# Attention masks of a decoder trunk: added by VectorE in place in PSUM instead of by matmuls with an identity

## Chip, cores and metric

The kernel runs on one core of a Trainium2 chip. The metric is the time of one execution on the device in microseconds (us), lower is better. Engines are named as the profile names them: PE is TensorE (PEld its weight loads), DVE is VectorE, ACT is ScalarE, POOL is GpSimd, SP is SyncE, which issues the DMAs.

## What is computed

A decoder trunk of four layers on 256 tokens of width 1024, in float32. Each layer has a token mixer and a SwiGLU feed-forward, both between RMS norms with a residual. The mixers are differential attention (layers 0 and 3), stick-breaking attention (layer 1) and sliding-window attention with sinks (layer 2). Cut to what matters here, the masks:

```
# layers 0 and 3: two softmaxes per head, causal
sc = einsum('bqhcd,bkhcd->bhcqk', qb, k) * scale
p = softmax(where(kpos <= qpos, sc, -inf), axis=-1)
wts = p[:, :, 0] - lam * p[:, :, 1]

# layer 1: stick-breaking, strictly causal
z = einsum('bqhd,bkhd->bhqk', qb, k) * scale
log_1m_beta = where(kpos < qpos, log_sigmoid(-z), 0.0)
suffix = cumsum(log_1m_beta, reverse=True) - log_1m_beta
a = where(kpos < qpos, exp(log_sigmoid(z) + suffix), 0.0)

# layer 2: a window of 128 keys, with a sink per head in the denominator
sc = where(in the window and in the sequence, sc, -inf)
m = maximum(max(sc), sink);  p = exp(sc - m)
probs = p / (sum(p) + exp(sink - m))
```

## The kernel before

**Streams.** The 256 tokens are two streams of 128 rows, `s` = 0 and 1, each a Python generator that goes through all layers (`stream`). Stream 1 attends to its own block of keys and to that of stream 0 (`nk = s + 1` blocks); stream 0 to its own alone.

**Weights.** Weights come from HBM in units of 128x1024 f32 (`load_dma`, tile `stage`). `split` makes two tiles of each: `hi` by ScalarE (rounded to f32r) and `lo` = stage - hi by VectorE. Projections multiply `hi` and `lo` by the split activations in three products (`project`, `rows_product`). Both streams use the same unit from a ring of 11; stream 0 may be at most 8 units ahead (`LAG`), and the splits are emitted 3 units ahead of use (`AHEAD`).

**The order of the work.** `Emitter` is a planner that writes the program in one order. It keeps a clock `em.t` that only matmuls and transposes advance (`mm`, `transpose`). A generator can yield `("d", ns)`: what follows is emitted only when that much TensorE work has been emitted, so the result of another engine is there by then. It can yield `("e", key)` to wait for an event and `("w",)` for a weight unit. Attention work is spawned as tasks (`turned`, `scores`, `values`, in layer 2 `keys` and `heads`) between the projections. From the first layer of stream 1 on, instructions are no longer kept in program order (`act.on = dve.on = pool.on = pe.on = False`), so each engine's final order may differ from the emitted one.

**A score step.** A step covers four score matrices, two `p` by two `j`, from queries and keys of 64 rows each. `score_banks` takes two PSUM banks of the stream (`tag="acc"`, two buffers), one for each `j`. `score_products` multiplies queries and keys for two `p`, all key blocks and both `j` (f32, 64 rows, 128 columns each) into them, then adds the mask. In PSUM, `start=True` on a bank's first matmul clears it, later ones add. The mask is 0 or -1e30 in bf16 (`masks`: causal, strict, before), and one bf16 matmul per bank and masked block with the identity `identb` adds it for both `p` at once. Layers 0, 1 and 3 mask only a stream's own block, layer 2 masks the other one too (`before`).

**After the scores.** In layers 0 and 3 VectorE takes the negated maximum (`nm`), ScalarE the exponentials with their sums (`e`, four instructions), VectorE combines the two softmaxes (`w`), TensorE transposes them (`tw`), ScalarE copies (`wT`), TensorE multiplies by the values (`pv`). In layer 1 ScalarE reads the scores directly with two sigmoids (`f`, `b`), VectorE scans and multiplies (`s`, `b`), TensorE transposes (`ta`). Layer 2 is like layer 0 with one softmax and a sink (`nm`, `es`, `e`, `l`, `tpr`, `pT`). The line that matters in all of them is the delay between a step and its transposes, 3500 ns in layers 0, 1 and 3, 6000 ns in layer 2.

Of the kernel before, what the change touches and what calls it, by code (L numbers as in the profile page):

```python
# [9 lines left out]
F32 = mybir.dt.float32  # L10
F32R = mybir.dt.float32r
BF16 = mybir.dt.bfloat16
I32 = mybir.dt.int32
AF = mybir.ActivationFunctionType
ALU = mybir.AluOpType
# [3 lines left out]
P = 128  # L19
# [138 lines left out]
def trunk_kernel(ctx, tc, x, positions, norm_gains, a_w_in, a_w_out, a_lambda, a_subln, b_w_in, b_w_out,  # L158
                 c_w_in, c_w_out, c_sinks, w_gate, w_up, w_down, out, depth=DEPTH):
    nc = tc.nc  # L160
    cst = ctx.enter_context(tc.tile_pool(name="cst", bufs=1))
# [6 lines left out]
    def bank(tag, s, shape, name):  # L168
        return ps.tile(shape, F32, tag=f"{tag}{s}", name=name, bufs=BANKS[tag])
# [16 lines left out]
    act, dve, pool, pe = (Start(e) for e in (nc.scalar, nc.vector, nc.gpsimd, nc.tensor))  # L186
# [106 lines left out]
    pool.memset(mhalf, -0.5)  # L293
    ident = cst.tile([P, P], F32, name="ident")
    make_identity(nc, ident)
    identb = cst.tile([P, P], BF16, name="identb")
    pool.tensor_copy(identb, ident)

    masks = {n: cst.tile([P, P], BF16, name=f"mask_{n}") for n in ("causal", "strict", "before")}
    for n, op, sign in (("causal", ALU.is_ge, 1), ("strict", ALU.is_gt, 1), ("before", ALU.is_gt, -1)):  # L300
# [72 lines left out]
    def mm(o, a, b, start, stop, f32=False):  # L373
        pe.matmul(o, a, b, start=start, stop=stop)
        n = 1
        for d in o.shape[1:]:
            n *= d
        em.t += n * COLUMN_NS * (4 if f32 else 1)
# [6 lines left out]
    def transpose(o, i):  # L385
        pe.transpose(o, i, ident)
        em.t += P * COLUMN_NS * 4
# [157 lines left out]
    def score_banks(s, n, name):  # L545
        return [bank("acc", s, [P, 2, n], f"sc_{name}{j}") for j in range(2)]

    def score_products(s, sc, q, k, mask):

        for p in range(2):  # L550
            for kb in range(s + 1):
                for j in range(2):
                    hs = slice(64 * j, 64 * j + 64)
                    mm(sc[j][:, p, kb * P:(kb + 1) * P], q(p)[hs], k(p, kb)[hs], p == 0 and kb == 0, False, True)
        for j in range(2):
            kbs = [kb for kb in range(s + 1) if mask(kb) is not None]
            for kb in kbs:
                mm(sc[j][:, :, kb * P:(kb + 1) * P], identb, mask(kb).unsqueeze(1).to_broadcast([P, 2, P]), False, kb == kbs[-1])

    def two_groups(s, name):  # L560
        return [[wk.tile([P, 4, P], F32R, tag=f"o{p}{s}", name=f"o{p}_{name}{g}") for p in "hl"] for g in range(2)]
# [11 lines left out]
    def layer_a(s, i, xn):  # L573
        inst = i // 3
        name = f"a{i}{s}"
# [18 lines left out]
        def scores(g):  # L594
            yield ("e", (name, "q", g))
            if s:
                yield ("e", (f"a{i}0", "k", g))
            yield ("d", 700)
            wT[g] = wk.tile([P, 4, nk, P], F32, tag=f"wT{s}", name=f"wT_{name}{g}", bufs=1)
            l = st[g] = sm.tile([P, 2, 4], F32, tag=f"l{s}", name=f"l_{name}{g}", bufs=2)  # L600
            el = st[g, "el"] = sm.tile([P, 4], F32, tag=f"el{s}", name=f"el_{name}{g}", bufs=2)
            ws = {}
            for step in range(3):
                if step < 2:
                    h0 = 2 * step
                    hs = slice(h0, h0 + 2)
                    sc = score_banks(s, nk * P, f"{name}{g}{h0}")
                    score_products(s, sc, lambda p: qT[g][:, h0 + p, :], lambda p, kb: kT[g, kb][:, h0 + p, :],
                                   lambda kb: masks["causal"] if kb == s else None)
                    nm = sm.tile([P, 2, 2], F32, tag=f"nm{s}", name=f"nm_{name}{g}{h0}")  # L610
                    e = [wk.tile([P, 2, nk * P], F32, tag="t2k", name=f"e{c}_{name}{g}{h0}", bufs=TMP) for c in range(2)]
                    if step:
                        em.set((name, "s", g))
                    for c in range(2):
                        dve.tensor_reduce(nm[:, c, :], sc[c], AX.X, ALU.max, negate=True)
                    for c in range(2):
                        for h in range(2):
                            act.activation(e[c][:, h, :], sc[c][:, h, :], AF.Exp, bias=nm[:, c, h:h + 1],
                                                 accum_out=l[:, c, h0 + h:h0 + h + 1])
                    r = sm.tile([P, 2], F32, tag=f"rl{s}", name=f"rl_{name}{g}{h0}")  # L620
                    dve.reciprocal(r, l[:, 1, hs])
                    dve.scalar_tensor_tensor(r, r, nlam[:, inst:inst + 1], l[:, 0, hs], ALU.mult, ALU.mult)
                    w = ws[step] = wk.tile([P, 2, nk * P], F32, tag=f"as{s}", name=f"w_{name}{g}{h0}", bufs=STEPS)
                    for h in range(2):
                        dve.scalar_tensor_tensor(w[:, h, :], e[1][:, h, :], r[:, h:h + 1], e[0][:, h, :], ALU.mult, ALU.add)
                    yield ("d", 3500)
                if step > 0:
                    if step == 2:
                        yield ("d", 1500)
                    tp = bank("tp", s, [P, 2, nk, P], f"tw_{name}{g}{step}")  # L630
                    for h in range(2):
                        for kb in range(nk):
                            transpose(tp[:, h, kb, :], ws[step - 1][:, h, kb * P:(kb + 1) * P])
                    act.activation(wT[g][:, 2 * step - 2:2 * step], tp, AF.Copy)
                    yield ("d", 300)
            lv = l[:, 0, :]
            dve.scalar_tensor_tensor(el, lv, EPS, lv, ALU.mult, ALU.mult)
            em.set((name, "w", g))
# [41 lines left out]
    def layer_b(s, i, xn):  # L680
        name = f"b{i}{s}"
# [19 lines left out]
        def scores(g):  # L701
            yield ("e", (name, "q", g))
            if s:
                yield ("e", (f"b{i}0", "k", g))
            yield ("d", 700)
            aT[g] = wk.tile([P, 4, 2, nk, P], F32, tag=f"wT{s}", name=f"aT_{name}{g}", bufs=1)
            as_ = {}
            for step in range(3):
                if step < 2:
                    p0 = 2 * step  # L710
                    sc = score_banks(s, n, f"{name}{g}{p0}")
                    score_products(s, sc, lambda p: qT[g][:, p0 + p, :], lambda p, kb: kT[g, kb][:, p0 + p, :],
                                   lambda kb: masks["strict"] if kb == s else None)
                    b, f, sm = [], [], []
                    for j in range(2):
                        f.append(wk.tile([P, 2, n], F32, tag="t2k", name=f"f{j}_{name}{g}{p0}", bufs=TMP))
                        sm.append(wk.tile([P, 2, n], F32, tag="t2k", name=f"s{j}_{name}{g}{p0}", bufs=TMP))
                        b.append(wk.tile([P, 2, n], F32, tag=f"as{s}", name=f"b{j}_{name}{g}{p0}", bufs=STEPS))
                        pool.memset(f[j][:, :, n - 1:n], 0.0)
                    for j in range(2):  # L720
                        act.activation(f[j][:, :, 0:n - 1], sc[j][:, :, 1:n], AF.Sigmoid, scale=-SCALE)
                        act.activation(b[j], sc[j], AF.Sigmoid, scale=SCALE)
                    for j in range(2):
                        for p in (1, 0):
                            dve.tensor_tensor_scan(sm[j][:, p, ::-1], f[j][:, p, ::-1],
                                                         reset[:, 256 - n:256][:, ::-1], 0.0, ALU.mult, ALU.max)
                        dve.tensor_tensor(b[j], b[j], sm[j], ALU.mult)
                    as_[step] = b
                    if step:
                        em.set((name, "s", g))  # L730
                    yield ("d", 3500)
                if step > 0:
                    if step == 2:
                        yield ("d", 1500)
                    for p in range(2):
                        tp = bank("tp", s, [P, 2, nk, P], f"ta_{name}{g}{2 * step - 2 + p}")
                        for j in range(2):
                            for kb in range(nk):
                                transpose(tp[:, j, kb, :], as_[step - 1][j][:, p, kb * P:(kb + 1) * P])
                        act.activation(aT[g][:, 2 * step - 2 + p], tp, AF.Copy)  # L740
                        yield ("d", 300)
            em.set((name, "w", g))
# [31 lines left out]
    def layer_c(s, i, xn):  # L774
        name = f"c{i}{s}"
# [18 lines left out]
        def heads(chunk, g):  # L794
# [13 lines left out]
            sc = score_banks(s, n, f"{name}{g}")  # L808
# [18 lines left out]
            dve.reciprocal(l, l)  # L827
            for j in range(2):
                dve.tensor_tensor(e[j], e[j], l[:, j, :].unsqueeze(2).to_broadcast([P, 2, n]), ALU.mult)
            yield ("d", 6000)  # L830
            for p in range(2):
                tp = bank("tp", s, [P, 2, nk, P], f"tpr_{name}{g}{p}")
                for j in range(2):
# [119 lines left out]
```

## Time and profile before

| | |
|---|---|
| time, median of 3 runs | 1204.88 us (1204.61 to 1205.26) |
| profiled execution, time | 1205.73 us |
| profiled execution, span | 1203.9 us |
| instructions | 16738 |
| granted TensorE clock | 0.998 of full speed |
| PE busy | 1185.8 us |
| DVE busy | 779.2 us |
| ACT busy | 656.9 us |
| POOL busy | 48.1 us |
| HBM read | 203.76 MB |

The span runs from the first to the last instruction of the program; the execution's own time is 1.83 us longer. Busy times are sums over the whole span. Matmuls are pipelined, and their ends in the profile are modelled, so a matmul's cost is better read from the distance between starts than from its own length. The helper that issues the instructions has one line (L181), so instructions are told apart by the tiles that they write and read: `sc_a<-mask_causal,identb` is a mask matmul in layers 0 and 3, where the letter after the underscore is the kind of layer.

### The profile page before, as it was taken

What the parts mean: (1) busy time and instruction counts of PE and PEld (TensorE: products, weight loads), DVE (VectorE), ACT (ScalarE), POOL (GpSimd) and SP (SyncE); (2) the same over time, 40 slices, a digit from 0 to 9 for tenths busy, and PEclk for the clock granted to TensorE, in tenths of its full rate; (3) what the DMA queues carried; (4) which work ended last, traced back from release to release, by engine and by line L of the source; (5) the groups of instructions that cost most, each with busy time, mean ns of one, the idle gap of its engine ahead of it and who ended that gap; (6) DMA issues with size and microseconds to landing.
All of it is one profiled execution on the core that took longest, in us unless ns stands there. A gap on an engine that the chain in (4) does not pass through costs nothing.

```text
span 1203.9 us, 16738 instructions
## 1 busy us (share of the span) xinstructions
PE 1185.8 (98%) x6028; PEld 971.6 (81%) x6028; DVE 779.2 (65%) x1217; ACT 656.9 (55%) x1197; POOL 48.1 (4%) x141
## 2 busy tenths in 40 slices
PE   8999999999999999999999999999999999999997
PEld 7787888888878888888888778888888788888886
DVE  7876765555847666555588666655587776655553
ACT  5665644444756665444476655444475565544442
POOL 2000100000200000000000000000010001000000
PEclk9999999999999999999999999999999999999999
DMA  8635465565644546656664246555565453566550
GB/s 280 206 120 159 151 192 186 189 192 179 225 139 123 176 140 193 191 181 189 192 199 135 88 144 191 191 189 187 185 205 156 129 175 123 179 189 192 180 170 35
DMA packets 140838, 205.90 MB, mean 171 GB/s; under 512 B 9554, under 2 KB 104916, under 8 KB 140756
## 3 DMA queue, kind: packets, MB, share of 16 engines
q1 hardware_dynamic: 140048, 204.51, 54.0%
q8 instruction: 47, 0.77, 0.3%
q10 hardware_dynamic: 708, 0.34, 0.1%
q14 instruction: 35, 0.29, 0.1%
HBM read 203.76 MB, written 1.05 MB: 170 GB/s over the span
## 4 chain that ended last, share of the span: by engine, by line
PE 90%; DVE 3%; ACT 3%; issue 2%; POOL 1%; DMA 1%; ACTq 0%; DVEq 0%; POOLq 0%
PE mm_f L181 39%; PE acc_f L181 18%; PE acc_a L181 3%; PE mm_c L181 2%; PE acc_b L181 2%; PE sc_a L181 2%; PE th_f L181 2%; DVE lo L181 1%; PE acc_c L181 1%; PE sc_b L181 1%; DMA stage<-in_a_w_in_dram 1%; ACT hi L181 1%; PE pv_a L181 1%; PE sc_c L181 1%; PE pv_c L181 1%
## 5 line engine op out<-in xcount | busy, mean ns | idle before, releaser
L181 DVE TENSOR_TENSOR lo<-stage,hi 128x1024 fp32r<-128x1024 f32 x378 | 461.0, 1223 | 285.5 <-ACT hi L181 283.6
L181 ACT ACTIVATE hi<-stage 128x1024 fp32r<-128x1024 f32 x378 | 399.5, 1061 | 324.1 <-PE mm_f L181 154.4
L181 PE MATMUL mm_f<-hi,xh_q 128*128 128x512 f32 x704 | 280.2, 398 | 0.0
L181 PE MATMUL mm_f<-lo,xh_q 128*128 128x512 f32 x704 | 274.5, 390 | 0.0
L181 PE MATMUL mm_f<-hi,xl_q 128*128 128x512 f32 x704 | 217.4, 390 | 1.0 <-DVE xl_q L181 1.0
L181 PEld LDWEIGHTS mm_f<-hi,xl_q 128*128 128x128 f32 x704 | 132.2, 188 | 30.4 <-DVE xl_q L181 1.9
L181 PEld LDWEIGHTS mm_f<-hi,xh_q 128*128 128x128 f32 x704 | 132.2, 188 | 26.1 <-ACT xh_q L181 0.2
L181 PEld LDWEIGHTS mm_f<-lo,xh_q 128*128 128x128 f32 x704 | 132.4, 188 | 25.8
L181 PE MATMUL acc_f<-hi,hTh_f 128*128 128x512 f32 x352 | 113.7, 399 | 0.5 <-ACT hTh_f L181 0.5
L181 PE MATMUL acc_f<-hi,hTl_f 128*128 128x512 f32 x352 | 111.4, 392 | 0.5 <-DVE hTl_f L181 0.4
L181 PE MATMUL acc_f<-lo,hTh_f 128*128 128x512 f32 x352 | 110.7, 390 | 0.0
L181 ACT ACTIVATE t_f<-mm_f,half_f 128x256 f32<-128x256 f32 x88 | 41.7, 474 | 79.7 <-PE mm_f L181 79.7
L181 PEld LDWEIGHTS acc_f<-hi,hTl_f 128*128 128x128 f32 x352 | 65.9, 188 | 14.9 <-DVE hTl_f L181 1.0
L181 PEld LDWEIGHTS acc_f<-lo,hTh_f 128*128 128x128 f32 x352 | 66.1, 188 | 14.0
L181 PEld LDWEIGHTS acc_f<-hi,hTh_f 128*128 128x128 f32 x352 | 63.7, 188 | 11.9 <-ACT hTh_f L181 0.8
L181 DVE SCALAR_TENSOR_TENSOR t_f<-t_f,mm_f 128x256 f32<-128x256 f32 x88 | 36.7, 417 | 35.2 <-ACT t_f L181 35.1
L181 DVE SCALAR_TENSOR_TENSOR h_f<-t_f,hsq_f,mm_f 128x256 f32<-128x256 f32 x88 | 42.3, 480 | 2.7
L181 ACT ACTIVATE hTh_f<-th_f 128x256 fp32r<-128x256 f32 x88 | 33.0, 375 | 17.0 <-PE th_f L181 16.7
L181 DVE TENSOR_TENSOR hTl_f<-th_f,hTh_f 128x256 fp32r<-128x256 f32 x88 | 36.5, 418 | 5.6 <-ACT hTh_f L181 5.3
L181 ACT ACTIVATE e_a<-sc_a,nm_a 128x128 f32<-128x128 f32 (+1 forms) x64 | 26.0, 420 | 17.1 <-DVE nm_a L181 16.9
L181 PE MATMUL th_f<-ident,h_f 128*128 128x128 f32 x176 | 33.5, 271 | 0.0
L181 PEld LDWEIGHTS th_f<-ident,h_f 128*128 128x128 f32 x176 | 24.1, 139 | 11.4 <-DVE h_f L181 0.3
(584 smaller groups left out, 1543.1 us busy)
## 6 DMA issues: line engine op xcount, KB each, us to landing
stage<-in_ffn_w_gate_dram SPq DMA_DIRECT2D x176, 256.0 KB, 2.9
stage<-in_ffn_w_up_dram SPq DMA_DIRECT2D x176, 256.0 KB, 3.1
stage<-in_ffn_w_down_dram SPq DMA_DIRECT2D x88, 512.0 KB, 3.5
stage<-in_a_w_in_dram SPq DMA_DIRECT2D x48, 512.0 KB, 3.8
stage<-in_b_w_in_dram SPq DMA_DIRECT2D x24, 512.0 KB, 3.6
stage<-in_a_w_out_dram SPq DMA_DIRECT2D x16, 512.0 KB, 3.9
stage<-in_c_w_in_dram SPq DMA_DIRECT2D x10, 512.0 KB, 3.6
gain<-in_norm_gains_dram SPq DMA_DIRECT2D x8, 512.0 KB, 4.1
```

The costliest lines, as they stand in the source:

```text
L181: i = call(*args, **kw)
```

## The change

The identity in bf16, `identb`, and the cast that makes it go; a pad of the same size keeps the addresses of what follows. The last score matmul of a bank now ends its group (`stop`), and VectorE adds the mask to the scores in PSUM, in place, one instruction per bank and masked block, with the mask broadcast over the two `p`. The planner's delays between a score step and its transposes grow by 800 ns.

```
-    identb = cst.tile([P, P], BF16, name="identb")
-    pool.tensor_copy(identb, ident)
+    cst.tile([P, 64], F32, name="pad")
...
             for kb in range(s + 1):
                 for j in range(2):
                     hs = slice(64 * j, 64 * j + 64)
-                    mm(sc[j][:, p, kb * P:(kb + 1) * P], q(p)[hs], k(p, kb)[hs], p == 0 and kb == 0, False, True)
+                    mm(sc[j][:, p, kb * P:(kb + 1) * P], q(p)[hs], k(p, kb)[hs], p == 0 and kb == 0, p == 1 and kb == s, True)
         for j in range(2):
-            kbs = [kb for kb in range(s + 1) if mask(kb) is not None]
-            for kb in kbs:
-                mm(sc[j][:, :, kb * P:(kb + 1) * P], identb, mask(kb).unsqueeze(1).to_broadcast([P, 2, P]), False, kb == kbs[-1])
+            for kb in range(s + 1):
+                if mask(kb) is not None:
+                    part = sc[j][:, :, kb * P:(kb + 1) * P]
+                    dve.tensor_tensor(part, part, mask(kb).unsqueeze(1).to_broadcast([P, 2, P]), ALU.add)
...
# layer_a, scores                                # layer_b, scores
-                    yield ("d", 3500)
+                    yield ("d", 4300)
...
# layer_c, heads
-            yield ("d", 6000)
+            yield ("d", 6800)
```

More of the change, by code (lines that the diff above doesn't have):

```diff
@@ L730, in scores @@
                         em.set((name, "s", g))
-                    yield ("d", 3500)
+                    yield ("d", 4300)
                 if step > 0:
```

## The prediction

> **What bounds the kernel now.** I read the shares of the engines first, then the chain that ended last, then the stretches of the four attention layers, and only then single instructions of the masks.
>
> ```profile
> PE 1185.8 (98%) x6028; PEld 971.6 (81%) x6028; DVE 779.2 (65%) x1217; ACT 656.9 (55%) x1197; POOL 48.1 (4%) x141
> PE 90%; DVE 3%; ACT 3%; issue 2%; POOL 1%; DMA 1%; ACTq 0%; DVEq 0%; POOLq 0%
> ```
>
> The first line is the busy time of each engine, the second the shares of the chain that ended last. TensorE is busy for all but 18 us and carries nine tenths of the chain, so a matmul taken away should shorten the kernel, unless what replaces it is waited for. VectorE, which gets the work, has a third of its time free on average, but the average hides the stages. The stretches of the layers (us, then busy us and instructions of PE, PEld, DVE, ACT, POOL, the granted clock, the DMA share, GB/s), where all masks lie:
>
> ```profile
> 30.00:130.00 100.00, 96.76 (x538) 77.20 (x538) 73.48 (x127) 63.91 (x163) 5.75 (x8) 1.00 0.51 157
> 330.00:430.00 100.00, 100.00 (x618) 80.54 (x617) 62.30 (x95) 64.75 (x112) 2.87 (x16) 1.00 0.45 141
> 630.00:700.00 70.00, 69.31 (x569) 59.32 (x569) 53.97 (x134) 47.42 (x137) 2.81 (x6) 1.00 0.33 103
> 930.00:1010.00 80.00, 79.62 (x452) 64.57 (x451) 57.80 (x102) 49.71 (x128) 5.71 (x8) 1.00 0.44 136
> ```
>
> These are layer 0 (differential), 1 (stick-breaking), 2 (sliding window) and 3 (differential). TensorE is the bound in each, at full clock. VectorE is at 73%, 62%, 77% and 72%, so layer 2 is where it has least room.
>
> **Removed: the mask matmuls.** The rows of the tile `identb` count them (durations min/median/max in ns):
>
> ```profile
> L181 PEld LDWEIGHTS <-identb x72: 95/98/100, 38.8 to 984.9; 128*128 128x128 bf16 x72
> L181 PE MATMUL sc_a<-mask_causal,identb x32: 272/278/283, 38.8 to 985.0; 128*128 128x256 bf16 x32
> L181 PE MATMUL sc_b<-mask_strict,identb x16: 272/278/284, 337.6 to 410.7; 128*128 128x256 bf16 x16
> L181 PE MATMUL sc_c<-mask_causal,identb x16: 272/273/283, 637.0 to 682.0; 128*128 128x256 bf16 x16
> L181 PE MATMUL sc_c<-mask_before,identb x8: 273/278/283, 647.5 to 681.9; 128*128 128x256 bf16 x8
> ```
>
> That is 72 matmuls in 32 score steps: 28 steps have a pair, and the four steps of stream 1 in layer 2 have four. Their 0.27 us each is no price, because matmuls overlap. What a pair costs shows only in the spacing of what stands around it. The trace also has score runs that were broken off without a mask behind them, so both cases can be read. In the timeline of TensorE (start, length):
>
> ```profile
> 63.10 0.71 PE L181 MATMUL sc_a<-kT_a,qT_a 64*128 64x128 f32 x4
> 63.74 0.39 PE L181 MATMUL sc_a<-mask_causal,identb 128*128 128x256 bf16 x2
> 63.89 0.47 PE L181 MATMUL mm_a001k<-hi,xh_n 128*128 128x512 f32 x1
> 64.20 0.39 PE L181 MATMUL mm_a001k<-lo,xh_n 128*128 128x512 f32 x1
> ...
> 936.48 0.48 PE L181 MATMUL sc_a<-kT_a,qT_a 64*128 64x128 f32 x2
> 936.89 0.50 PE L181 MATMUL mm_a310v<-hi,xh_n 128*128 128x512 f32 x1
> 937.23 0.39 PE L181 MATMUL mm_a310v<-lo,xh_n 128*128 128x512 f32 x1
> ```
>
> With a pair, the scores end at 63.10 + 0.71 = 63.81 and the second projection matmul starts at 64.20, 0.39 later. Without, the scores end at 936.96 and the second one starts at 937.23, 0.27 later. A pair before projection matmuls is worth 0.12 us, not the 0.22 that its own two starts suggest: part of the switch from 64-row scores to full-array matmuls is paid either way. The same comparison where transposes follow:
>
> ```profile
> 38.19 0.72 PE L181 MATMUL sc_a<-kT_a,qT_a 64*128 64x128 f32 x8 [0.78 <-ACT kT_a L181]
> 38.84 0.39 PE L181 MATMUL sc_a<-mask_causal,identb 128*128 128x256 bf16 x2
> 39.06 0.60 PE L181 MATMUL tt_a010q<-ident,t_a010q 128*128 128x128 f32 x4
> 39.42 0.47 PE L181 MATMUL mm_a000v<-hi,xl_n 128*128 128x512 f32 x1
> ...
> 977.06 0.48 PE L181 MATMUL sc_a<-kT_a,qT_a 64*128 64x128 f32 x2
> 977.47 0.66 PE L181 MATMUL tt_a311k<-ident,t_a311k 128*128 128x128 f32 x4
> 977.89 0.48 PE L181 MATMUL mm_a311v<-hi,xh_n 128*128 128x512 f32 x1
> ```
>
> With a pair 39.42 - 38.91 = 0.51, without 977.89 - 977.54 = 0.35: worth 0.16 us. The pair itself took 39.06 - 38.84 = 0.22, so 0.06 comes back in the switch. And the last of four masks in a row:
>
> ```profile
> 668.21 0.27 PE L181 MATMUL sc_c<-mask_causal,identb 128*128 128x256 bf16 x1
> 668.32 0.38 PE L181 MATMUL tpr_c<-ident,e_c 128*128 128x128 f32 x2
> ```
>
> It takes 668.32 - 668.21 = 0.11, so four take 0.44; less the same 0.06, 0.38. In the timeline 22 of the 28 pairs are followed by projection matmuls and 6 by transposes or value products. The gain of TensorE is 22 x 0.12 + 6 x 0.16 + 4 x 0.38 = 2.6 + 1.0 + 1.5 = 5.1 us. Its bounds: the full spacing of all masks, 36 x 0.22 = 7.9 us, above; 36 x 0.12 = 4.3 us below, and not less, since TensorE issues strictly less than before.
>
> **Added: 72 VectorE adds in place in PSUM,** 128x256 f32 with a bf16 mask broadcast over two heads. No row of before writes PSUM from VectorE. The nearest rows read PSUM at the same size, the first as a plain two-operand instruction:
>
> ```profile
> L181 DVE TENSOR_TENSOR hTl_f<-th_f,hTh_f 128x256 fp32r<-128x256 f32 x88 | 36.5, 418 | 5.6 <-ACT hTh_f L181 5.3
> L181 DVE SCALAR_TENSOR_TENSOR h_f<-t_f,hsq_f,mm_f 128x256 f32<-128x256 f32 x88 | 42.3, 480 | 2.7
> 639.18 0.42 DVE L181 TENSOR_TENSOR t_c201q<-mm_c,crq_c 128x256 f32<-128x256 f32 x1
> 639.52 0.15 DVE L181 TENSOR_TENSOR es_c<-nm_c,nsink 128x4 f32<-128x4 f32 x1
> ```
>
> I take 0.42 us long and 0.34 from start to start (639.52 - 639.18); the bounds are that 0.34 and 0.48 for the dearer form. That is 72 x 0.34 = 24 us more of VectorE time, 30 us by the busy sum. Two adds stand ahead of a step's reductions and lengthen the score chain by 0.68 us (four: 1.36). TensorE finishes the scores 0.22 earlier, so the softmax starts 0.46 us later per step, 0.91 for four masks. The planner's delays grow by 800 ns at the same points, so that much more TensorE work is emitted before the transposes that need the result.
>
> What hides this, and who waits:
>
> ```profile
> ACT f_b L181 <- PE sc_b L181: 2.8, 5, 1.6
> ...
> PEld sc_a L181 <- ACT e_a L181: 1.8, 5, 0.6
> ```
>
> These are waits (total us, times, longest). No row among TensorE's waits names the products `w_a` or `b_b`: the transposes behind the softmax have never waited for VectorE, so 0.46 us is covered there. What is late is the score bank: each stream has two, a step uses both, and the next step's scores wait for the exponentials (the second row, 5 times). At 5 places 0.46 us more is 2.3 us at most; I take half, 1.2 us, since other TensorE work can be ordered in. In layers 0, 2 and 3 VectorE's reduction is the first reader of the scores, so the wait for them only moves to the add. In layer 1 it is new on VectorE: ScalarE waited there (first row), and now the weight splits `lo` queue behind the waiting add, and the projections behind the splits, 0.6 us a time by that row's mean. Splits are made three units ahead of use (`AHEAD`), so I cost this at nothing; without that cover it is 2.8 us, the row's whole sum.
>
> VectorE's tightest stretch is the start of layer 2:
>
> ```profile
> 635.00:640.00 5.00, 5.00 (x46) 4.73 (x46) 4.39 (x12) 3.37 (x8) 0.00 (x0) 1.00 0.34 105
> 640.00:645.00 5.00, 5.00 (x46) 4.70 (x46) 5.00 (x14) 3.76 (x12) 0.00 (x0) 1.00 0.75 248
> 645.00:650.00 5.00, 5.00 (x52) 4.31 (x51) 4.84 (x13) 2.58 (x12) 0.00 (x0) 1.00 0.60 187
> ```
>
> It is busy 14.2 of 15 us. Two steps with a pair and one with four masks fall here: 8 x 0.34 = 2.7 us into 0.8 us of room, so about 2 us of backlog, worked off after 650. Queued behind it are rotary products that feed transposes of queries. I take 0.8 us of it as lost on TensorE (nothing if the order is re-planned, 2 us if all of it is felt).
>
> **Edits at nothing:** the cast that made `identb` goes from GpSimd's first microseconds, where nothing waits for it; the pad keeps 64 x 4 = 128 x 2 bytes, so addresses stay; the moved stop flag adds no instruction; no DMA is touched.
>
> **Sum.** The profiled execution took 1205.73 us, 1.83 of it around its span of 1203.9; it is 0.85 above the median 1204.88. From it: 1205.73 - 5.1 + 1.2 + 0.8 = 1202.6, and against the median 1204.88 - 3.1 = **1201.8 us**.
>
> **Rivals.** (1) *The score banks eat the gain.* The wait for the exponentials is felt in full at those 5 places and layer 2's backlog in full: 2.3 + 2 = 4.3, net 0.8 us faster, 1204.1. That is no change, since 0.2%, 2.4 us, is about the least that a measurement of this kernel can tell. For it: the five waits. Against: these sum to only 1.8 us, and in the stretches of layers 1 and 3 above TensorE stood still for 0.0 and 0.4 us.
>
> (2) *Slower: every second score step waits for its banks.* One mechanism, in the 32 steps: if the later softmax pushes the scores of 16 of them by the full 0.68 us, 10.9 us are lost against 5.1, and it comes to 1204.88 + 5.8 = 1210.7. It decides from 8 steps on (8 x 0.68 = 5.4). For it: within a layer the two steps of a group follow each other closely and share the banks. Against: only 5 waited so far.
>
> (3) *Weight loads are the limit, not matmuls.* PEld is busy 81%, and a mask's load has a row of 98 ns; if the two of a pair overlap, the pair takes 0.10 us of the load path. If only loads count, 36 x 0.10 = 3.6 us go, less 2.0 for the longer score chain: 1204.88 - 1.6 = 1203.3, no change. Against: in the rows above, matmuls of 512 columns follow each other at 0.31 and 0.34 us, well above 98 ns. The Trainium skill, page "Trainium Kernel Development and Optimization", section "Performance Expectations", says that busy time of matmuls is a bad measure of the limit because they are pipelined, and that the share of LDWEIGHTS is a good one. By that rule the 98% proves little; the trace agrees in part, since 0.06 of the 0.22 us of a pair comes back in the switch.
>
> (4) *The full gain is kept:* 1204.88 - 5.1 = 1199.8, if re-planning hides all of the added chain.
>
> **How the numbers follow.** The forecast has 0.42, (4) 0.15, (1) 0.20, (3) 0.09, (2) 0.14. Faster by over 0.2% are the forecast and (4), together 0.57, less a little of the forecast's upper side: 0.56. Same: (1), (3) and that rest, 0.30. Slower: (2), 0.14. The range runs from 1198.5 (a gain of 6.4, near the middle of 5.1 and 7.9, with nothing lost) to 1206.0 (rival (1) with the split waits of 2.8 us mostly felt); rival (2) is left out above. The forecast's own range is 1200.2 to 1203.0.
>
> **What would show it.** Right: no matmul reads a mask; 72 adds at about 0.42 us write the score banks; TensorE's busy time falls by about 5 us and its idle time rises by about 2; the stretch of layer 1 shortens most cleanly. Wrong: new waits of `sc_a`, `sc_b` or `sc_c` for `e_a`, `f_b` or `e_c` beyond some 4 us; `tpr_c` or `tq_c` waiting for VectorE in layer 2; adds far above 0.48 us; or TensorE's order so changed that the feed-forward stages too differ in length.

## The result and the profile after

The changed kernel takes 1208.46 us (median of 6 runs, 1207.60 to 1210.36) against 1204.89 (1204.61 to 1205.26) before: a ratio of 1.0032 over the runs (1.0030 by the two medians), 95% interval 1.0019 to 1.0044. It is 3.6 us slower; the forecast was 1201.8, 3.1 us faster. The profiled execution took 1210.36 us, its span 1208.3, so it lies 1.9 above the median.

The busy time of each engine and the shares of the chain that ended last:

```profile
PE 1184.4 (98%) x5956; PEld 969.0 (80%) x5956; DVE 801.2 (66%) x1289; ACT 656.6 (54%) x1197; POOL 47.7 (4%) x140
PE 88%; DVE 4%; ACT 3%; issue 2%; POOL 1%; DMA 1%; ACTq 0%; DVEq 0%; POOLq 0%
```

72 matmuls went and 72 VectorE instructions came. TensorE's busy time fell by 1.4 us only, though some 7 were taken away, as will be seen. Most of the instructions that replaced them (min/median/max in ns):

```profile
L181 DVE TENSOR_TENSOR sc_a<-sc_a,mask_causal x32: 420/423/433, 38.9 to 990.6; 128x256 f32<-128x256 f32 x32
```

That is the 0.42 us that was forecast. The stretches of layers 2 and 3 (us, busy us and instructions of PE, PEld, DVE, ACT, POOL, granted clock, DMA share, GB/s):

```profile
630.00:700.00 70.00, 66.66 (x516) 55.92 (x515) 59.10 (x147) 44.44 (x131) 1.66 (x4) 0.98 0.34 107
930.00:1010.00 80.00, 75.63 (x412) 60.80 (x410) 58.72 (x107) 48.10 (x130) 5.07 (x7) 0.96 0.44 136
```

TensorE, busy for 69.31 and 79.62 us there before, now stands still for 3.3 and 4.4 us, and its clock is no longer 1.00 throughout. The longest waits of TensorE (total us, times, longest):

```profile
PE mm_a310v L181 <- DVE t_a310k L181: 2.9, 1, 2.9
PE tq_c L181 <- ACT pT_c L181: 1.7, 1, 1.7
...
PE acc_c L181 <- ACT e_c L181: 1.0, 1, 1.0
```

The first was 0.4 before, the others were not there. To see what each place costs, take the last start of a gate and up matmul (`mm_f`) in each layer: 311.93, 614.40, 884.46 and 1188.33 us before. The table has the change of each layer, from the difference of these times between a kernel's profile and that of before; the experiments are described below.

| kernel | layer 0 | layer 1 | layer 2 | layer 3 | median against before |
|---|---|---|---|---|---|
| after | -3.56 | -0.53 | +2.14 | +6.03 | +3.57 |
| e1 | -1.74 | -0.21 | +4.42 | -0.53 | +2.36 |
| e2 | -2.79 | -0.26 | -1.31 | +4.96 | +1.16 |
| e3 | -1.91 | -0.21 | +0.02 | -0.60 | -0.87 |
| e4 | -1.05 | -0.91 | -4.02 | -0.83 | -7.30 |
| e5 | -0.86 | -0.21 | +0.03 | -0.52 | -1.81 |
| e6 | -3.11 | -0.63 | +2.38 | -0.62 | -2.06 |
| e7 | -3.38 | -0.63 | -1.22 | -0.49 | -4.93 |
| e8 | -3.32 | -0.26 | -1.15 | -0.41 | -4.08 |
| e9 | -0.89 | -0.95 | -0.06 | -1.17 | -2.83 |
| e10 | -3.20 | -0.51 | +2.16 | -0.61 | -2.19 |
| e11 | -3.32 | -0.53 | +0.93 | -0.63 | -2.40 |
| e12 | -2.92 | -0.53 | +0.93 | -0.66 | -2.39 |

Layer 0's column also holds the start of the kernel, which differs from profile to profile: when the last matmul of the first projection, `mm_a000q`, starts (19.16 us before), these profiles already lie between 0.96 us ahead (e11) and 0.73 behind (e2). So up to about 1 us of that column, either way, is chance. Each row is one profiled execution, and some lie far from their medians: that of e3 took 1203.07 us, 1.24 below its median, that of e4 1198.92, 1.04 above. The changed kernel gained 4.1 us in layers 0 and 1 and lost 8.2 in layers 2 and 3.

**Layer 3, one stall.** Rows of the timeline there (start, length, engine, in brackets the idle time before and who ended it; rows between them are left out), first of the kernel before, then of the changed one:

```profile
927.95 1.05 PE L181 MATMUL pv_a<-V_a,wT_a 128*128 128x128 f32 x8
...
931.12 0.62 PE L181 MATMUL mm_a310k<-hi,xl_n 128*128 128x512 f32 x2
931.67 0.69 DVE L181 TENSOR_TENSOR on_a<-pv_a,os_a 128x512 f32<-128x512 f32 x1 [1.13 <-POOL os_a L181]
...
932.87 0.68 DVE L181 TENSOR_TENSOR t_a310k<-mm_a310k,srk_a 128x512 f32<-128x512 f32 x1
933.70 0.47 PE L181 MATMUL mm_a310v<-hi,xh_n 128*128 128x512 f32 x1 [0.38 <-DVE t_a310k L181]
```

```profile
928.52 1.05 PE L181 MATMUL pv_a<-V_a,wT_a 128*128 128x128 f32 x8
...
930.88 0.49 PE L181 MATMUL sc_a<-kT_a,qT_a 64*128 64x128 f32 x4
931.19 1.02 POOL L181 TENSOR_TENSOR os_a<-os_a,mhalf 128x4 f32<-128x4 f32 x1 [31.82 <-DVE os_a L181]
932.24 0.69 DVE L181 TENSOR_TENSOR on_a<-pv_a,os_a 128x512 f32<-128x512 f32 x1 [1.13 <-POOL os_a L181]
...
933.44 0.68 DVE L181 TENSOR_TENSOR t_a310k<-mm_a310k,srk_a 128x512 f32<-128x512 f32 x1
934.27 0.77 PE L181 MATMUL mm_a310v<-hi,xh_n 128*128 128x512 f32 x1 [2.90 <-DVE t_a310k L181]
...
935.26 0.63 PE L181 MATMUL mm_a310v<-hi,xh_n 128*128 128x512 f32 x1
935.69 0.63 PE L181 MATMUL mm_a310v<-lo,xh_n 128*128 128x512 f32 x1
```

The projection `mm_a310v` needs the stream's only `mm` bank, which the two rotary products `t_a310k` read before. These stand behind `on_a` in VectorE's queue, and `on_a`, the scaled value products `pv_a`, waits 1.13 us for GpSimd's power. All this is the same in the kernel before, and in both kernels `mm_a310v` starts 5.75 us after `pv_a`. What differs is what TensorE has to do in these 5.75 us. Before, `pv_a` itself, three groups of six projection matmuls (`mm_a301q`, the last of `mm_a310k`, `mm_a301q`) and two transposes keep it busy for 5.37 us, and it waits 0.38. Now two of the three groups run ahead of `pv_a`; with one group and four score matmuls behind it the work lasts 2.85 us, and TensorE waits 2.90. The last of `mm_a310k` ended at 928.69, so VectorE stood idle for 1.13 us although the rotary products could have run. (Before, it ended at 931.74, when `on_a` had just started, so there the order in the queue cost little.) No mask is in this chain. And the stall is followed by a slow clock, in stretches of 5 us:

```profile
930.00:935.00 5.00, 2.10 (x11) 1.41 (x10) 3.87 (x7) 0.81 (x7) 1.02 (x1) 0.86 0.57 181
935.00:940.00 5.00, 5.00 (x17) 3.92 (x16) 2.84 (x4) 1.55 (x2) 0.00 (x0) 0.50 0.00 0
940.00:945.00 5.00, 4.90 (x31) 3.65 (x30) 2.58 (x5) 1.83 (x3) 0.00 (x0) 0.96 0.38 105
```

In 935 to 940 TensorE counts as busy throughout but issued 17 matmuls where the kernel before issued 37.

**Layer 2, a longer chain.** The step with four masks, from its adds to the transposes `tq_c` that wait for the bank (picked rows):

```profile
644.48 0.42 DVE L181 TENSOR_TENSOR sc_c<-sc_c,mask_before 128x256 f32<-128x256 f32 x1
...
646.29 0.42 DVE L181 TENSOR_TENSOR sc_c<-sc_c,mask_causal 128x256 f32<-128x256 f32 x1
646.62 1.27 DVE L181 TENSOR_REDUCE nm_c<-sc_c 128x2 f32<-128x512 f32 x2
648.15 0.15 DVE L181 TENSOR_TENSOR nm_c<-nm_c,nsink 128x4 f32<-128x4 f32 x1
648.59 1.06 ACT L181 ACTIVATE hi<-stage 128x1024 fp32r<-128x1024 f32 x1 [3.65 <-PE mm_c L181]
649.55 0.46 ACT L181 ACTIVATE e_c<-sc_c,nm_c 128x256 f32<-128x256 f32 x1
651.44 0.39 ACT L181 ACTIVATE pT_c<-tpr_c 128x256 f32<-128x256 f32 x1
651.89 0.44 PE L181 MATMUL tq_c<-ident,t_c202q 128*128 128x128 f32 x2 [1.69 <-ACT pT_c L181]
```

The four adds and what is queued between them take VectorE from 644.48 to 646.62. The maximum is ready at 648.30. ScalarE has a weight split `hi` ahead of the exponentials, which had itself waited 3.65 us for a projection, and the copy `pT_c` that frees the bank comes last.

### The profile page after: what moved, and what is told of

It reads as the page before. It is cut to its first block, busy times and chain, and to the rows that moved or that the text cites. A ratio compares the mean times of both kernels' runs of the same rounds, so it can differ in the third digit from the quotient of the medians.

```text
span 1208.3 us, 16666 instructions
## 1 busy us (share of the span) xinstructions
PE 1184.4 (98%) x5956; PEld 969.0 (80%) x5956; DVE 801.2 (66%) x1289; ACT 656.6 (54%) x1197; POOL 47.7 (4%) x140
## 3 DMA queue, kind: packets, MB, share of 16 engines
HBM read 203.76 MB, written 1.05 MB: 169 GB/s over the span
## 4 chain that ended last, share of the span: by engine, by line
PE 88%; DVE 4%; ACT 3%; issue 2%; POOL 1%; DMA 1%; ACTq 0%; DVEq 0%; POOLq 0%
PE mm_f L181 39%; PE acc_f L181 18%; PE acc_a L181 3%; PE mm_c L181 2%; PE acc_c L181 2%; PE acc_b L181 2%; DVE lo L181 2%; PE th_f L181 2%; ACT hi L181 1%; PE sc_a L181 1%; DMA stage<-in_a_w_in_dram 1%; PE sc_c L181 1%; PE pv_a L181 1%; PE pv_c L181 1%; PE tp_q L181 1%
```

## The experiments

Two theories were set against each other: (1) the planner's longer delays cost the time, through the order they give; (2) the adds cost it. In the end the first answered for layer 3 and the second for layer 2.

**First four runs: delays and adds apart.** e1 is the changed kernel with the old delays.

```
-                    yield ("d", 4300)        # layers 0, 3 and 1
+                    yield ("d", 3500)
-            yield ("d", 6800)                # layer 2
+            yield ("d", 6000)
```

> The changed kernel with the planner's delays put back to 3500/3500/6000 ns; the adds stay on VectorE. Theory 1 (the longer delays emit the value products of layer 3 so late that VectorE's on_a stands ahead of the rotary products that free the bank of the next projection): the 2.9 us wait of mm_a310v for t_a310k goes and layer 3 no longer loses 6.3 us; layers 0 and 1 keep their 4.1, layer 2 keeps its loss of 2.1: about 1202.3 us (1200.5 to 1204). Theory 2 (the adds themselves lengthen VectorE's chain, in layers 2 and 3): the delays matter little, about 1208.5 us, and the wait for t_a310k stays at 2 us or more.

1207.54 us (1204.75 to 1208.60), ratio 1.0014 (1.0006 to 1.0023). Layer 3 came out as theory 1 had it, the wait for `t_a310k` back at 0.4 us; the total did not, and lies nearer to theory 2's: layers 0 and 1 kept only 1.95 of their 4.1 us, and layer 2 lost 4.4 instead of 2.1. A second stall had come at its end, in the rows of TensorE's waits and of two stretches:

```profile
PE acc_c L181 <- ACT e_c L181: 2.0, 1, 2.0
```

```profile
690.00:695.00 5.00, 3.05 (x11) 2.14 (x10) 4.93 (x13) 4.21 (x14) 0.87 (x2) 0.87 0.00 0
695.00:700.00 5.00, 5.00 (x26) 4.05 (x26) 2.51 (x7) 3.37 (x10) 0.92 (x2) 0.79 0.13 41
```

e2 is the reverse, the mask matmuls of before with the long delays (the diff above, upside down, on the kernel before).

> The kernel before, with its mask matmuls on TensorE, and only the planner's delays raised to 4300/4300/6800 ns. Theory 1 (delays): the order of layer 3 becomes that of the changed kernel, TensorE waits 2 to 3 us for a rotary product there and the granted clock falls after it: about 1210 us (1208 to 1212). Theory 2 (adds): without adds the delays only give more cover, 1204.9 us (1204 to 1206) with granted clock near 1.00 in the stretch of layer 3.

1206.34 us (1204.63 to 1209.35), ratio 1.0011 (1.0002 to 1.0020). Neither figure was met, but the places decide: without a single add, layer 3 lost 5.0 us by the same stall (`mm_a310v` for `t_a310k`, 2.9 us, with the same order on TensorE as in the changed kernel), and the layers before it gained 4.4 by the delays, which neither theory had said. The stretches:

```profile
930.00:935.00 5.00, 2.86 (x7) 2.21 (x8) 4.37 (x7) 0.00 (x0) 0.07 (x1) 0.69 0.33 102
935.00:940.00 5.00, 4.90 (x36) 3.83 (x35) 2.09 (x3) 2.91 (x5) 0.00 (x0) 0.97 0.29 80
```

e3 is the pure exchange: the adds, old delays, and the planner's clock advanced as the matmuls would have done it.

```
                    dve.tensor_tensor(part, part, mask(kb).unsqueeze(1).to_broadcast([P, 2, P]), ALU.add)
+                    em.t += 2 * P * COLUMN_NS
```

> The changed kernel with delays of 3500/3500/6000 ns, and the planner's clock is advanced by the 107 ns that each removed mask matmul would have taken, so that everything is emitted in the order of the kernel before: the pure exchange of 72 matmuls for 72 adds. Theory 1 (order): close to the forecast, 1201.8 us (1200 to 1203.5), no TensorE wait over 2 us in layer 3. Theory 2 (adds): 1207 us or more, with waits on VectorE in layers 2 and 3 of 2 us or more each.

1204.31 us (1202.99 to 1205.92), ratio 0.9995 (0.9986 to 1.0004): no change, between both theories. e4 is e3 without its adds, so without any mask.

```
-                    dve.tensor_tensor(part, part, mask(kb).unsqueeze(1).to_broadcast([P, 2, P]), ALU.add)
```

> As the kernel before, but the masks are left out altogether, neither matmul nor add (attention is computed unmasked), with the planner's clock advanced as if they were there: the emitted order is that of before. It measures the term of TensorE alone. By the forecast's term, 5.1 us (4.3 to 7.9): 1199.8 us (1197 to 1200.6). If weight loads were the limit: 3.6 us, 1201.3 us. If the place of the masks is mostly covered by other waits: within 1 us of 1204.9. What e3 takes more than this one is the price of the 72 adds: theory 1 says 2 us or less, theory 2 says 5 us or more.

1197.88 us (1197.78 to 1198.92), ratio 0.9943 (0.9931 to 0.9956). The mask matmuls are worth 7.3 us, not 5.1, and the adds cost 1204.31 - 1197.88 = 6.4 us, not 2.0. By the table, which has the two profiled executions, the adds cost 4.0 us in layer 2 (+0.02 against -4.02), 0.7 in layer 1 and 0.2 in layer 3, and in layer 0 the run with adds is 0.9 ahead, which its start does not explain: 4.1 in all. The other 2.3 us are the distance of these two executions from their medians, 1.24 and 1.04, and can't be put down to a layer. The chain of layer 2's four-mask step in e4, to be held against that of the changed kernel:

```profile
646.37 0.68 DVE L181 TENSOR_REDUCE nm_c<-sc_c 128x2 f32<-128x512 f32 x1
648.30 0.15 DVE L181 TENSOR_TENSOR nm_c<-nm_c,nsink 128x4 f32<-128x4 f32 x1
648.48 0.47 ACT L181 ACTIVATE e_c<-sc_c,nm_c 128x256 f32<-128x256 f32 x1 [2.04 <-DVE nm_c L181]
650.39 0.39 ACT L181 ACTIVATE pT_c<-tpr_c 128x256 f32<-128x256 f32 x1
650.84 0.43 PE L181 MATMUL tq_c<-ident,t_c202q 128*128 128x128 f32 x2
```

The scores of this step start at 644.20 here and at 642.53 in the changed kernel. So `pT_c` comes 6.2 us after them without masks and 8.9 us after them with the adds: 2.7 us more, twice the 1.36 us that four adds take by themselves. Of these, 1.5 lie ahead of the maximum (ready at 648.45 here) and 1.2 between it and the first exponential, where `hi` runs in the changed kernel. `tq_c` does not wait here. In e9 below, which keeps e4's emitted order and adds these masks, the chain is again 8.9 us long and `tq_c` waits 1.7. That `hi` and the bank carry the delay on is read from these timelines; no run changed them by themselves.

**Layer 2 by itself.** e5 is e3 with layer 2's masks as matmuls again; e9 is e4 with the adds of layer 2 alone, layers 0, 1 and 3 unmasked. `HOW` is a table by layer.

```
+                if how == "pe":
+                    mm(part, identb, m, False, kb == kbs[-1])
+                elif how == "dve":
+                    dve.tensor_tensor(part, part, m, ALU.add)
# e5: HOW = {0: 'dve', 1: 'dve', 2: 'pe', 3: 'dve'}; e9: {0: 'none', 1: 'none', 2: 'dve', 3: 'none'}
```

> As the pure exchange (e3: delays of 3500/3500/6000 ns, emitted order of before), but layer 2 keeps its mask matmuls on TensorE; layers 0, 1 and 3 have their adds on VectorE. Theory A (the adds cost in layer 2 alone, where VectorE is full: without any masks layer 2 was 4.0 us shorter, with adds 0.0): the run without masks, 1197.9, plus 4.0 us for layer 2's matmuls plus about 1 us for the other adds: 1202.5 us (1201.5 to 1203.5), with TensorE busy at least 4.7 of 5 us in 650 to 655 where e3 has 3.0, and runs closer together than e3's 1203.0 to 1205.9. Rival (all adds cost alike, 6.4 us over 72, so 4.3 us for the 48 of layers 0, 1 and 3): 1206 us.

> As the run without masks (e4, 1197.9 us, emitted order of before), but layer 2 has its 24 adds on VectorE; layers 0, 1 and 3 are computed unmasked. If the adds cost in layer 2 because VectorE is full there: 1197.9 + 3.7 to 4.9 (e3's 6.4 less what e5 leaves for the others): 1202 us (1201 to 1203.5), with TensorE busy 3.0 of 5 us in 650 to 655. If all 72 adds cost alike, 24/72 of 6.4: 1200.0 us.

e5: 1203.37 us (1202.78 to 1204.16), ratio 0.9983 (0.9974 to 0.9992). e9: 1202.36 us (1201.51 to 1203.66), ratio 0.9976 (0.9967 to 0.9985). Both met what was expected of layer 2. Its 24 adds cost 1202.36 - 1197.88 = 4.5 us, 0.19 each; the other 48 leave about 2. Not all of it is standing still: from the last `mm_f` of layer 1 to that of layer 2 TensorE is idle for 2.79 us in e9 and for 1.23 in e4, so 1.6 of the table's 4.0 us. The rest is the same 1465 matmuls starting further apart in another order, which was not followed up. The stretch from 650 to 655 in e9 and then in e5:

```profile
650.00:655.00 5.00, 3.01 (x24) 2.60 (x23) 4.22 (x14) 4.17 (x13) 0.00 (x0) 1.00 0.17 52
```

```profile
650.00:655.00 5.00, 4.93 (x42) 4.40 (x41) 4.00 (x11) 4.02 (x13) 0.00 (x0) 1.00 0.08 28
```

**Layer 3 by itself.** e6 is the changed kernel with layer 3's delay alone put back.

```
+DELAY = {0: 4300, 1: 4300, 2: 6800, 3: 3500}
...
-                    yield ("d", 4300)
+                    yield ("d", DELAY[i])
```

> The changed kernel with one number put back: the delay of layer 3 is 3500 ns, those of layers 0, 1 and 2 stay at 4300, 4300 and 6800. Theory 1 (layer 3's loss is the longer delay there): the wait of mm_a310v for t_a310k falls from 2.9 us below 1, the clock stays at 1.00 in the stretch of layer 3, and of its loss of 6.3 us at least 5 come back: 1203 us (1202 to 1204.5). Theory 2 (the adds of layer 3): 1207.5 us or more.

1203.12 us (1202.00 to 1203.97), ratio 0.9981 (0.9972 to 0.9990), as theory 1 had it. The wait:

```profile
PE mm_a310v L183 <- DVE t_a310k L183: 0.4, 1, 0.4
```

VectorE's queue did not change for that. It still has `on_a` ahead of the rotary products, with the same wait; TensorE again has the three groups of projection matmuls between `pv_a` and `mm_a310v`:

```profile
930.04 0.69 DVE L183 TENSOR_TENSOR on_a<-pv_a,os_a 128x512 f32<-128x512 f32 x1 [1.13 <-POOL os_a L183]
```

e10 keeps all the long delays and only moves layer 3's `on_a` in VectorE's queue.

```
+            late = 600 if i == 3 else 0
+            if late:
+                yield ("d", late)
             on = wk.tile([P, 4, P], F32, tag="t2k", name=f"on_{name}{g}", bufs=TMP)
             dve.tensor_tensor(on, o, ss.unsqueeze(2).to_broadcast([P, 4, P]), ALU.mult)
-            yield ("d", 4200)
+            yield ("d", 4200 - late)
```

> The changed kernel with all its delays; in layer 3 alone the scaling on_a is emitted 600 ns later and its transposes follow at the same place, so that the rotary products of the next keys, t_a310k, stand ahead of on_a in VectorE's queue instead of behind it. If the stall of layer 3 is this head of the line (VectorE waits for on_a's input while t_a310k could run): the wait of mm_a310v for t_a310k falls from 2.9 us below 1, the clock stays at 1.00 behind it, and the time is 1203.5 us (1202.5 to 1205), near e6. If the later value products are at fault by themselves, or VectorE's load: 1207.5 us or more.

1203.00 us (1201.77 to 1204.12), ratio 0.9979 (0.9971 to 0.9988): against the kernel before 5.8 us come back, as 5.6 did with e6, with every delay as in the changed kernel. VectorE's timeline shows the rotary products ahead of `on_a`, and the stretch has TensorE busy throughout at full clock:

```profile
929.13 0.69 DVE L181 TENSOR_TENSOR t_a310k<-mm_a310k,crk_a 128x512 f32<-128x512 f32 x1 [0.65 <-PE mm_a310k L181]
929.74 0.68 DVE L181 TENSOR_TENSOR t_a310k<-mm_a310k,srk_a 128x512 f32<-128x512 f32 x1
...
933.14 0.69 DVE L181 TENSOR_TENSOR on_a<-pv_a,os_a 128x512 f32<-128x512 f32 x1 [0.91 <-POOL os_a L181]
```

```profile
930.00:935.00 5.00, 5.00 (x30) 3.74 (x31) 4.09 (x8) 2.77 (x11) 1.40 (x1) 1.00 0.60 197
```

Here too TensorE has only one group of matmuls between `pv_a` and `mm_a310v`, but the bank is free when it comes. So the stall takes two things: value products that TensorE runs two groups later among the projections, which is what the longer delay does, and `on_a` ahead of the rotary products in VectorE's queue, which was so before. Taking away either one, as e6 and e10 do, takes away the stall.

**Versions made from the findings.** e7 has adds in layers 0, 1 and 3, matmuls in layer 2, and the delays of e6. e8 has matmuls everywhere and the delays of e6.

```
# e7: HOW = {0: 'dve', 1: 'dve', 2: 'pe', 3: 'dve'}; e8: all 'pe'
# both: DELAY = {0: 4300, 1: 4300, 2: 6800, 3: 3500}
```

> A version made from both findings: mask matmuls on TensorE in layer 2, adds on VectorE in layers 0, 1 and 3, and the delays of the changed kernel but for layer 3's, which is 3500 ns. If the two losses are layer 2's adds and layer 3's delay, and the longer delays help elsewhere (e2 was 4.4 us ahead at the end of layer 2 with matmuls and longer delays): 1204.9 - 4.4 - 1 = 1199.5 us (1198.5 to 1201.5). If longer delays and adds do not go together: 1202.5 us, as e5.

> The kernel before, all masks as matmuls, with the delays of the changed kernel but for layer 3's, which stays at 3500 ns. It separates e7's gain: e2, with all delays longer, was 4.4 us ahead at the end of layer 2 in its profiled run and lost 5.0 in layer 3. If that lead is real and the loss is the delay of layer 3: 1200.5 us (1199.5 to 1202). If the lead is an accident of one run: 1204.9 us.

e7: 1200.25 us (1200.01 to 1200.69), ratio 0.9958 (0.9945 to 0.9970), faster than both kernels. e8: 1201.10 us (1200.59 to 1201.34), ratio 0.9964 (0.9952 to 0.9977). So the lead of e2 was real: 4.1 of e7's 4.9 us are the longer delays of the first three layers; why they gain was not pursued. The masks on VectorE add 0.85, less than the two intervals can tell apart, though the runs of e7 and e8 hardly overlap.

**Relieving VectorE in layer 2.** e11 is e6 with one rotary instruction of the queries on GpSimd, e12 is e7 with the same.

```
-            dve.tensor_tensor(o, t1, t2, ALU.add)
+            (pool if pooled else dve).tensor_tensor(o, t1, t2, ALU.add)     # pooled for layer 2's queries
```

> e6 (all 72 adds on VectorE, layer 3's delay 3500 ns, the others long), with the last of the three rotary instructions of layer 2's queries (128x256, 0.34 us from start to start, 8 of them) moved from VectorE to GpSimd, which is 4% busy. If layer 2 loses because VectorE is full there: the stall in 650 to 655 shrinks (TensorE busy at least 4 of 5), and of the 3.6 us by which e6 falls behind e7 in layer 2 most comes back: 1200.5 us (1199 to 1202). If the loss in layer 2 is the longer chain of each step, whatever VectorE's load: 1203 us, as e6.

> Control for e11: e7 (mask matmuls in layer 2, adds elsewhere) with the same move of a rotary instruction to GpSimd in layer 2. VectorE has room there without the adds, so the move should be worth little: 1200.25 us, within 0.7. If it gains as much as in e11, e11's gain says nothing about the adds.

e11: 1202.79 us (1202.15 to 1203.61), ratio 0.9979 (0.9971 to 0.9988), no better than e6: by its time the rival, 1203, came true and not the 1200.5 of a full VectorE. e12, the control: 1202.80 us (1202.48 to 1203.27), ratio 0.9980 (0.9971 to 0.9989), 2.5 slower than e7, where no change was expected. The move has a price of its own, shown by picked rows of e11's timeline:

```profile
629.74 0.73 POOL L183 TENSOR_TENSOR t_c200q<-t_c200q 128x256 f32<-128x256 f32 x1
...
636.48 1.22 DVE L183 TENSOR_TENSOR lo<-stage,hi 128x1024 fp32r<-128x1024 f32 x1
636.64 1.63 POOL L183 TENSOR_TENSOR t_c201q<-t_c201q 128x256 f32<-128x256 f32 x1 [6.17 <-DVE t_c201q L183]
638.33 0.44 PE L183 MATMUL tq_c<-ident,t_c201q 128*128 128x128 f32 x2 [0.72 <-POOL t_c201q L183]
638.55 1.59 POOL L183 TENSOR_TENSOR t_c210q<-t_c210q 128x256 f32<-128x256 f32 x1 [0.27 <-DVE t_c210q L183]
639.45 0.71 DVE L183 TENSOR_TENSOR l_c<-l_c,es_c 128x4 f32<-128x4 f32 x1
```

With the move, adds and matmuls cost the same in layer 2: it stands at +0.93 us both with adds (e11) and with matmuls (e12); without it, at +2.38 (e6) and -1.22 (e7). The stall shrinks as well, and the clock stays up:

```profile
650.00:655.00 5.00, 4.33 (x39) 3.42 (x37) 4.59 (x9) 4.13 (x12) 2.89 (x2) 1.00 0.33 105
```

So the two runs do not decide between VectorE's load and the longer chain of each step: the sign of the first (the smaller stall) and the time of the second both came, and the move's own price, which changes the order too, may cover what the adds cost. That the adds of layer 2 cost 4.5 us is shown by e9, and e5 agrees; by which of the two is left open. What would take work from VectorE there at no price was not tried.

## Why the prediction was wrong, step by step

The way from the kernel before to the changed one, run by run: 7.3 us gained on TensorE (e4), 6.4 lost to the adds (e3 against e4), 1.2 gained by the other delays and the planner's clock (e6 against e3), 5.6 lost to layer 3's delay (after against e6): -7.3 + 6.4 - 1.2 + 5.6 = +3.5. These are differences of neighbouring runs, so they must add up to the measured +3.57 but for rounding; the sum says how large each part is and proves none. The smallest, 1.2, is between runs whose ranges overlap.

- **The step that failed** is the sentence on the planner's delays, that they grow "so that much more TensorE work is emitted before the transposes". It counted as cover at no cost. But a delay of a score step also delays all that the task emits after it, down to the value products. In layer 3 these came two groups of projection matmuls later, so that TensorE had 2.85 instead of 5.37 us of work to cover the 5.75 us from `pv_a` to the free `mm` bank. (The expectation of e1 has VectorE's order changed by the delay; the traces show it unchanged.) The prediction asked what is queued behind the adds, but not what the delayed task holds up. This was worth 5.6 us: without it the change is 2.1 us faster than before (e6), not 3.6 slower. That e6 comes near the forecast's 3.1 is in part luck, since TensorE's gain and the cost of the adds, below, were both taken too small, and these errors cancel in part.
- **TensorE's gain** was 5.1 and measured 7.3 us (6.8 in the profile of e4). In layers 0, 1 and 3, 1.05, 0.9 and 0.8 us were gained where 8 pairs by 0.12 or 0.16 make about 1.0 (layer 0's is within the chance of its start): the discount for the switch holds, and in all the upper bound of 7.9 held. In layer 2 it was 4.0, where the forecast had 2.0 (four pairs and four times 0.38). The distances from start to start behind the 24 mask matmuls sum to 2.8 us in the profile before, and those behind the feed-forward's matmuls `mm_f` fell by 0.9, most of it a wait of 0.6 us for `xl_q` that e4 does not have.
- **Layer 2's backlog** was taken at 0.8, bounded by 0 and 2, and came to 4.0 to 4.5. The backlog of VectorE was read rightly: in the changed kernel it is busy for all 15 us from 635 to 650. What was missed, as far as the timelines show, is what stands behind the delayed maximum on ScalarE: a split `hi` that gets ahead of the exponentials, and behind these the copy that frees the transposes' bank. The bound was a backlog on one engine, not the path over three. The idle time of this path is 1.6 us of the 4.0; how the rest comes about stays open.
- **The score banks** were taken at 1.2 us, in the row of `sc_a` for `e_a`. That wait fell instead, from 1.8 us in 5 to 0.8 in 2:

```profile
PEld sc_a L181 <- ACT e_a L181: 0.8, 2, 0.4
```

But the same two banks also hold the output products (`acc_c`), and these waited for the exponentials: 1.0 us in the changed kernel and 2.0 in e1, in rows above, where the kernel before has no such wait. The bank was the right thing to look at, the row the wrong one.

- **Layer 1's splits** were taken at nothing. ScalarE did wait, 13.0 us in 7 places where it had been 2.8 in 5, but the adds cost only 0.7 us there (e3 against e4), so most of it was covered; that the three units ahead did this was not tested.

```profile
ACT f_b L181 <- DVE sc_b L181: 13.0, 7, 3.3
```

- **The adds' own length**, 0.42 us and 0.34 from start to start, was right.
- **The rivals.** Rival 2 has the sign and nearly the time (1210.7), by a mechanism that did not occur: the scores of layers 0 and 3 waited for the exponentials at 2 places, and the loss sits in layers 2 and 3; the near time is luck. Rival 1's time, 1204.1, is nearly that of the pure exchange (e3, 1204.31), but by terms of 7.3 and 6.4 where it had 5.1 and 4.3. Rival 3 had 3.6 us for TensorE's term; e4 shows 7.3, twice that. The Trainium skill ("Trainium Kernel Development and Optimization", "Performance Expectations") has the share of weight loads as the better measure; taken as a price of these matmuls, it came out too low here. Rivals 1 and 4 took over the forecast's silence on the delays. Among the signs named in advance, `tq_c` did wait in layer 2, though for ScalarE's copy and not for VectorE; and TensorE's idle time rose by 5.8 us where about 2 were named. None of them looked at layer 3.

## What to carry to other kernels

A delay in a planner is no mere cover: it moves every later instruction of the same task. For each chain that ends in a buffer being freed (here 5.75 us from `pv_a` to the bank), ask how much work is left between its start and the one who needs the buffer, and what stands waiting in the queues on the way. Price such an edit by itself, with the operations unchanged, before joining it to another: in the kernel with mask matmuls the longer delays were worth -4.1 us in three layers (e8) and +5.2 in the fourth (e2 against e8), more than the exchange of the masks. And where an engine is full, follow the delayed result over all engines to the buffer that it frees; the backlog on one engine is no upper bound.

## What the runs showed of the hardware

- **A stall can halve the granted clock after it.** After the 2.9 us stall the clock was 0.50 over 935 to 940, and matmuls of 512 columns started 0.43 us apart (935.26 to 935.69) instead of 0.23 (930.44 to 930.67 in the kernel before). In e2 the same stall gave 0.69 in 930 to 935 and 0.97 in 935 to 940. The record of the granted clock in the traces has only 1.00 and 0.50 there: 0.50 for 6.83 us from 933.58 in the changed kernel, for 3.41 us from 931.92 in e2. The 1.7 us stall of layer 2 was followed by 3.41 us at 0.50 in the changed kernel, e1, e6 and e10, and by none in e3 and e9. Both stalls are shorter than 3.41 us, and each 3.41 us at half the clock costs 1.7 us at most. The Trainium skill ("TensorE: Matmul & The Clock Gate", Part 1) describes a gate with two rates, half and full, set by the activity in a window of about 3.4 us that runs by itself. The 0.50 agrees, and so do the lengths of once and twice 3.41 us, and such a window would explain why one stall costs differently from run to run. It may be why runs with such stalls spread over 2.0 (e6) to 4.7 us (e2), and those of e5, e7, e8 and e12, without one, over 0.7 to 1.4; that was not tested by itself.
- **GpSimd and VectorE slow each other.** The same add of 128x256 took GpSimd 0.73 us at 629.74 in e11 and 1.63 us at 636.64, while VectorE subtracted `hi` from `stage`, both in SBUF; VectorE's add of 128x4, 0.16 us as a median, took 0.71 beside the next one. The Trainium skill ("Perfetto Trace Analysis", "Optimizing Scalar/DVE Operations") says that the two share a read port, so that moving work between them may not help. The runs agree that the move did not help: the control lost 2.5 us. Which port it was no run here shows.
